# A decoder block's attention stage: the third group's key projections done by seven products one stage sooner, the softmaxes queued behind the key splits

## Chip, core and metric

One core of a Trainium2 chip. The metric is the device time of one execution in microseconds. TensorE multiplies matrices, VectorE and ScalarE work element by element, GpSimd does a few side operations and issues some transfers, SyncE issues most transfers (DMA). Each of these engines runs its own queue in order; they wait for one another through semaphores.

## What is computed

One block of a decoder on 1024 tokens of width 1024, float32: an RMS norm with modulation, one wide projection, two token mixers beside each other (retention in chunks of 128 with 4 heads, and dilated window attention with 12 heads in three groups), gates that merge them, an MLP and a last norm. What matters here is the attention:

```python
ATT_GROUPS = ((128, 1), (512, 4), (2048, 16))      # window, dilation; 4 heads of 128 each
...
for gi, (win, dil) in enumerate(ATT_GROUPS):
    aq, ak, av = parts[4 + 3 * gi], parts[5 + 3 * gi], parts[6 + 3 * gi]
    o, lse = dilated_group(heads(aq, 4), heads(ak, 4), heads(av, 4), tab, win, dil)
...
wts = jax.nn.softmax(jnp.stack(lses, axis=0), axis=0)
att = jnp.einsum('gbhs,gbhsd->bshd', wts, o_all)
```

with `proj = h @ w_in` ahead of it, and in each group scores, a bias by distance, a softmax over the window, and the product with the values. The three groups' results are weighted by a softmax over their log denominators.

## The kernel before, in words

**Precision.** Every factor is split into a high and a low half (`split_w` L194, `k_split` L1484, `q_prep` L1475: ScalarE rounds the high half, VectorE subtracts it for the low half), and every product is made of three matmuls (`mm3` L203: high by low, low by high, high by high). A matmul of 128 x 128 by 512 columns is the unit.

**Stages.** First values; more values; `queries_keys` (L1212); values; the 32 chunks of retention, which also project its gates; the attention stage in two pairs of heads; then gates, output projections and the MLP.

**Seven products.** `queries_keys` projects pairs of 128-column blocks by the class `Blocks`: it works on a 2 x 2 partition of the matrices with seven products in place of eight (`ORDER` names them), each of 4 x 3 matmuls, so 84 matmuls for a pair. `PAIRS` (L1136) is the order of the pairs: r is a query or key of retention, a are two attention queries, g two gates. `a_load` (L1140) loads the weights, `a_out` (L1165) puts the results together and stores them to DRAM (`aq_d` for the queries). A plain projection, `proj_gen` (L477), takes 48 matmuls for one block.

**The attention stage.** A head is written (g, a): group g = 0, 1, 2 and head a = 0, 1 of the pair; pairs 0 and 1 follow each other. `combos` (L1751) gives the order (1,0), (1,1), (2,0), (2,1), (0,0), (0,1). In `att_step` (L1753), step i projects the keys of its head on TensorE and weaves into that, by `weave` (L493), the scores of the head before (`scores_gen` L1492; VectorE adds the bias and so empties the PSUM bank). Behind the step's matmuls come `k_split` for its keys and `scores_end` (L1526) for the head before: VectorE takes the maxima, ScalarE the exponentials of 8 blocks. Where a group is finished, `stats_out` (L1600) stores maxima and sums to DRAM and loads them back in another order.

Steps 6 to 9 are `cover_step` (L1791): a gate's plain projection covers other work. Step n = 0 (gate 0) takes the scores of (0,1), splits values, ends the softmax, makes the weights of the groups (`weights` L1608) and scales the probabilities of group 0 (`pscale` L1640); n = 1 (gate 1) is a projection alone; n = 2 (gate 2) weaves in transposes of the probabilities and the products with the values (`weave_pv` L1737). The first lines after each gate's matmuls copy its result out of PSUM, one half by VectorE (L1827), one by ScalarE (L1828). The PSUM pool for projections (`ps_mm`) has two buffers, which the steps take in turn, so gate 2 writes where gate 0 was; that for scores has four.

**What sets the order.** The schedule is the order of the Python calls: each engine queues its instructions as the program issues them. Loads are planned by `Steps` (L60 on): they go through three raw buffers, three ahead, and their `prep` (the splits) is put ahead of the body of the step before (`following` L114), or where a step's body calls for it ("late", or manual). `with_sums` (L576) puts a transfer that sums retention results, on GpSimd's queue, behind the second and sixth part of each projection. `u_final` (L680) scales and stores a retention head; the last is stored in the first attention step.

Of the kernel before, what the change touches and what calls it, by code (L numbers as in the profile page):

```python
# [140 lines left out]
def block_kernel(ctx, tc, io, stop=None, dbg=None):  # L141
# [433 lines left out]

    def with_sums(gen):  # L576

        return at(at(gen, 1, result_sum), 5, result_sum)

    hd = {}  # L580
    NG = H * NC
# [551 lines left out]
    r_pairs = [("r", t, h) for h in range(H) for t in "qk"]  # L1133
    a_pairs = [("a", g, p) for p in range(2) for g in range(3)]
    g_pairs = [("g", i) for i in range(len(GATES) // 2)]
    PAIRS = [{"r": r_pairs, "a": a_pairs, "g": g_pairs}[i].pop(0) for i in "rargrargrargrargaa"]  # L1136
    NA = len(PAIRS)
    OA = {}

    def a_load(q, part):  # L1140
        pair = PAIRS[q]
        src = io[{"g": "w_gate2", "a": "w_aq"}.get(pair[0]) or f"w_r{pair[1]}"]
# [22 lines left out]
    def a_out(q, n, x, y=None):  # L1165

        pair = PAIRS[q]
        if q not in OA:
            OA[q] = [x4(f"qa{q}{i}") for i in range(2)]
        i, t = int(n[0]) - 1, int(n[1]) - 1  # L1170
        o, view = OA[q][i][:, 512 * t:512 * t + 512], lambda z: z
        if pair[0] == "a" and pair[1] == 1:
            o = OA[q][i].rearrange("p (r n i) -> p r n i", r=4, n=2)[:, :, t, :]
            view = lambda z: z.rearrange("p (i r) -> p r i", r=4)
        elif pair[0] == "a" and pair[1] == 2:
            o = OA[q][i].rearrange("p (r i) -> p r i", r=8)[:, :, 64 * t:64 * t + 64]
            view = lambda z: z.rearrange("p (i r) -> p r i", r=8)
        f = AF.Sigmoid if pair[0] == "g" else AF.Copy
        if y is None:
            nc.scalar.activation(o, view(x), f)  # L1180
        else:
            (nc.vector.tensor_add if n == "12" else nc.vector.tensor_sub)(o, view(x), view(y))
            if pair[0] == "g":
                nc.scalar.activation(o, o, f)
        if n in ("12", "21"):
            if pair[0] == "g":
                dst = gate_d[GATES[2 * pair[1] + i]]
# [287 lines left out]
    def q_prep(pair, g, a):  # L1475
# [5 lines left out]
            A["q", g, a] = (hi, lo)  # L1481
        return prep

    def k_split(pair, g, a, ps):  # L1484

        hi, lo = ring(f"kh{pair}{g}{a}"), ring(f"kl{pair}{g}{a}")
        src, h_, l_ = by_blocks(ps, g), shaped(hi, g), shaped(lo, g)
        nc.scalar.copy(h_, src)
        nc.vector.tensor_sub(l_, src, fv(h_))
        A["k", g, a] = (hi, lo)  # L1490
# [109 lines left out]
    def stats_out(pair, g):  # L1600

        if g == 1:
            A["stn"] = A["p"].tile([P, 3, 8, 4], F32, tag="stn", name=f"stn{pair}")
        d = dram.tile([S, 4], F32, name=f"std{pair}{g}")
        nc.sync.dma_start(natural(d, g, 4), blocks(A["st"][:, g], g))
        nc.sync.dma_start(A["stn"][:, g], natural(d, 0, 4))

    def weights(pair):  # L1608

# [138 lines left out]
                done += 1  # L1748
        drain(main)

    combos = [(g, a) for g in (1, 2, 0) for a in range(2)]  # L1751

    def att_step(pair, i):  # L1753

        g, a = combos[i]

        def body(*args):
            ps = ps_mm(f"ak{pair}{i}")
            gen = with_sums(proj_gen(ps, args[-1]))
            if i == len(combos) - 2:  # L1760
                v_fetch(pair, 0)
            if i > 0:
                last = combos[i - 1]
                weave(gen, NK, scores_gen(pair, *last), len(SB[last[0]]), lag=2)
            elif pair == 0:
                args[0](1, True)
                for _ in range(4):
                    next(gen)
                on_T(H - 1, NC - 1)
                drain(gen)  # L1770
                u_final(H - 1)
                for h in range(H):
                    sums_left.extend(sums_of(h))
                open_att()
                args[0](3)
            else:

                gen = at(at(gen, 3, args[0]), NK - 1, lambda: k_split(pair, g, a, ps))
                weave_pv(gen, NK - 1, 0, 2)
            if i == 0:  # L1780
# [4 lines left out]
            if i > 0:  # L1785
                scores_end(pair, *last)
                if last[1] == 1:
                    stats_out(pair, last[0])
        return body

    def cover_step(pair, n):  # L1791
# [4 lines left out]
        def body(*args):  # L1796
            ps = ps_mm(f"gate0{i}")
            gen = with_sums(proj_gen(ps, args[-1]))
            if n == 0:
                v_fetch(pair, 1)  # L1800
                weave(gen, 6, scores_gen(pair, *combos[-1]), len(SB[0]), lag=2, rest=False)
                drain(gen)
                v_split(pair, 0, False)
                scores_end(pair, *combos[-1])
# [36 lines left out]
            nc.sync.dma_start(gate_d[i], t)  # L1841

    for pair in range(2):
        for i, (g, a) in enumerate(combos):
            steps.add(att_step(pair, i),
                      [wsplit(io["w_ak"][g * 4 + 2 * pair + a])] +
                      ([(aq_d[pair, *combos[i - 1]], q_prep(pair, *combos[i - 1]))] if i > 0 else []),
                      manual=("late" if pair else True) if i == 0 else False)
# [902 lines left out]
def pack(x, c, w_ada, b_ada, norm1_g, w_in, rel_bias, ret_gn_g, ret_gn_b,  # L2751
# [50 lines left out]
```

## Time and profile before

| | |
|---|---|
| three runs | 2182.73, 2183.21, 2183.33 us, median 2183.21 |
| profiled execution | 2182.64 us |
| its span, first to last instruction | 2180.9 us |
| granted TensorE clock, mean | 0.999 |
| stage of seven products | about 180 to 523 us of the span |
| attention stage, pair 0 | about 944 to 1090 us |
| attention stage, pair 1 | about 1091 to 1240 us |

Rows of the profile are read so: a line of kernel.py, an engine, an operation, the output tile, an arrow, the input tiles, shapes, a count, busy time or mean. In a timeline the first number is the start in us from the span's start, the second the time taken; brackets give the idle time before and what ended it. PE is TensorE, DVE VectorE, ACT ScalarE, POOL GpSimd, SP SyncE; a q behind the name is its queue issuing a transfer. Matmuls overlap in the pipeline, so their distance from start to start counts and not the 389 ns that one takes.

### The profile page before, as it was taken

Reading aid. Unit: us, or ns where it says so; the run is one execution under the profiler, and the core shown is the slowest. Engines: PE = TensorE matmul, PEld = TensorE weight load, DVE = VectorE, ACT = ScalarE, POOL = GpSimd, SP = SyncE. Lnnn points to the kernel's source line nnn. Section 1 sums busy time; section 2 is a strip of 40 time slices with the busy share of each in tenths; the row PEclk is TensorE's granted clock in tenths of the full one; section 3 lists DMA queues with packets and bytes.
Section 4 is the critical chain, followed back from the end, with each engine's and each line's share of the span. In section 5 each row is a group of like instructions: output and inputs, shape, how many; then the busy total and the mean of one; then the engine's idle time right before and its main releaser. Section 6 shows DMA issues by size and latency. Waiting matters only on the chain. (4 is left out here: it accounts for less than half of the span.)

```text
span 2180.9 us, 27323 instructions
## 1 busy us (share of the span) xinstructions
PE 2156.0 (99%) x10084; PEld 1791.6 (82%) x10084; DVE 1491.7 (68%) x2333; ACT 942.8 (43%) x1729; POOL 164.0 (8%) x195
## 2 busy tenths in 40 slices
PE   8999999999999999999999999999999999999998
PEld 6888888888878888888888888888778888888887
DVE  5985777774467877854655644776876665877855
ACT  5553323323434544544644625434454545533413
POOL 0001111100012212211100000001000000000003
PEclk9999999999999999999999999999999999999999
DMA  9859998844685555557763275654254435645322
GB/s 383 289 209 297 296 298 257 243 119 174 237 301 170 198 174 194 181 172 190 184 167 108 81 268 189 224 186 139 65 182 150 153 136 194 249 137 175 111 87 78
DMA packets 160881, 416.78 MB, mean 191 GB/s; under 512 B 27749, under 2 KB 55660, under 8 KB 157676
## 3 DMA queue, kind: packets, MB, share of 16 engines
q1 hardware_dynamic: 151416, 368.67, 47.9%
q0 software_dynamic: 9008, 46.14, 9.9%
q8 instruction: 79, 1.29, 0.2%
q14 instruction: 54, 0.44, 0.1%
q10 hardware_dynamic: 324, 0.23, 0.0%
HBM read 319.93 MB, written 156.13 MB: 218 GB/s over the span
## 5 line engine op out<-in xcount | busy, mean ns | idle before, releaser
L207 PE MATMUL qap<-hh,qaw 128*128 128x512 f32 x216 | 84.0, 389 | 0.0
L209 PE MATMUL qap<-hl,qaw 128*128 128x512 f32 x216 | 84.0, 389 | 0.0
L211 PE MATMUL qap<-hh,qaw 128*128 128x512 f32 x216 | 84.0, 389 | 0.0
L617 POOL TENSOR_TENSOR j<-qk,j 128x512 fp32r<-128x512 f32 x32 | 43.2, 1351 | 412.4 <-ACT j L616 393.8
L2122 POOL TENSOR_TENSOR accnf<-accnf,sqnf 128x256 f32<-128x256 f32 (+1 forms) x18 | 16.6, 922 | 609.9 <-ACT sqnf L2118 609.9
L2226 ACT ACTIVATE a<-a 128x512 f32<-128x512 f32 x48 | 30.3, 631 | 73.7 <-DVE a L2225 73.7
L1542 ACT ACTIVATE P<-P,ng 128x128 f32<-128x128 f32 (+1 forms) x96 | 42.0, 439 | 36.6 <-DVE ng L1539 36.6
L2434 ACT CAST w2h<-w2s 128x512 fp32r<-128x512 f32 x36 | 22.4, 622 | 78.7 <-DVE w2s L2472 78.7
L264 DVE TENSOR_TENSOR fw<-w1r,fw 128x512 fp32r<-128x512 f32 x48 | 32.9, 688 | 33.6 <-ACT fw L254 33.6
L1957 DVE TENSOR_TENSOR rwl<-rwl,rwh 128x1024 fp32r<-128x1024 f32 x25 | 30.2, 1220 | 29.1 <-ACT rwh L1987 29.1
L207 PE MATMUL fp<-h2h,fw 128*128 128x512 f32 x128 | 50.0, 391 | 0.0
L211 PE MATMUL fp<-h2h,fw 128*128 128x512 f32 x128 | 49.8, 389 | 0.0
L209 PE MATMUL fp<-h2l,fw 128*128 128x512 f32 x128 | 49.8, 389 | 0.0
L207 PE MATMUL roa<-rh,rwl 128*128 128x512 f32 x128 | 49.8, 389 | 0.0
L209 PE MATMUL roa<-rl,rwh 128*128 128x512 f32 x128 | 49.8, 389 | 0.0
L211 PE MATMUL roa<-rh,rwh 128*128 128x512 f32 x128 | 49.8, 389 | 0.0
L652 ACT COPY sm<-sT 128x128 f32<-128x128 f32 x32 | 8.5, 266 | 93.7 <-PE sT L640 93.7
L207 PEld LDWEIGHTS qap<-hh,qaw 128*128 128x128 f32 x216 | 40.5, 188 | 8.5
L209 PEld LDWEIGHTS qap<-hl,qaw 128*128 128x128 f32 x216 | 40.5, 188 | 8.4
L211 PEld LDWEIGHTS qap<-hh,qaw 128*128 128x128 f32 x216 | 40.5, 188 | 8.4
L2122 POOL TENSOR_TENSOR accn<-accn,sqn 128x512 f32<-128x512 f32 x12 | 15.5, 1293 | 386.1 <-ACT sqn L2118 386.1
L1947 ACT ACTIVATE rh<-rl 128x512 fp32r<-128x512 f32 x56 | 31.7, 623 | 23.4 <-PE roc L209 8.4
(3097 smaller groups left out, 7251.4 us busy)
## 6 DMA issues: line engine op xcount, KB each, us to landing
v<-vd SPq DMA_DIRECT2D x32, 512.0 KB, 4.5
raw<-in_w_ada_dram SPq DMA_DIRECT2D x32, 512.0 KB, 5.3
w1r<-in_w_ff_dram SPq DMA_DIRECT2D x32, 512.0 KB, 4.6
yt<-y POOLq DMA_DIRECT2D x24, 512.0 KB, 7.6
xsd<-as SPq DMA_DIRECT2D x24, 512.0 KB, 2.8
w2r<-in_w_ff2s_dram SPq DMA_DIRECT2D x24, 512.0 KB, 6.9
em<-in_w_ada_dram SPq DMA_DIRECT2D x16, 512.0 KB, 10.2
wrvs<-in_w_rv_dram POOLq DMA_DIRECT2D x16, 512.0 KB, 10.0
```

Source lines behind the costliest of these rows:

```text
L207: nc.tensor.matmul(o, wl, xh, start=first, stop=False, skip_group_check=skip)
L209: nc.tensor.matmul(o, wh, xl, start=False, stop=False, skip_group_check=skip)
L211: nc.tensor.matmul(o, wh, xh, start=False, stop=last, skip_group_check=skip)
L264: nc.vector.tensor_sub(t[:, 512:], src, fv(t[:, :512]))
L617: nc.gpsimd.tensor_sub(t[:, 1], src, fv(t[:, 0]))
L652: nc.scalar.copy(sm, ps[:, :C])
L1542: nc.scalar.activation(v, v, AF.Exp, bias=ng[:, blk:blk + 1], accum_out=st[:, g, blk, 2 + a:3 + a])
L1947: nc.scalar.activation(hi, fv(lo), AF.Copy, scale=sign)
L1957: nc.vector.tensor_sub(lo, fv(lo), fv(hi))
L2122: (nc.vector if f == 7 else nc.gpsimd).tensor_add(G["acc", key], G["acc", key], sq)
L2226: nc.scalar.activation(o, o, AF.Relu)
L2434: nc.scalar.copy(hi, src)
```

## The change

The keys of group 2 are no longer projected in the attention stage. Their weights are packed for seven products, two pairs (k) are put into `PAIRS`, and the results go to DRAM; the attention stage loads and splits them as it does queries. The keys of group 0 are now projected in two halves, `att_first` and `att_second`, each of four parts of the projection, and each half covers the scores of one head. `scores_end` of a head is called one step later than before, behind the loads' splits and the key split of the step (`scored`, `scores_done`). The statistics' store is issued by ScalarE, and the load back by SyncE one call later. The last four stores of retention go to GpSimd's queue, and three sums instead of two are issued in each projection.

```diff
     def with_sums(gen):
-        return at(at(gen, 1, result_sum), 5, result_sum)
+        return at(at(at(gen, 1, result_sum), 3, result_sum), 5, result_sum)
...
-    def u_final(h, es=range(4)):
+    def u_final(h, es=range(4), queue=nc.sync):
...
-            nc.sync.dma_start(y_d[h][:, 2 * (i % 2):2 * (i % 2) + 2, e // 2], t.rearrange("p (t x) -> p t x", t=2))
+            queue.dma_start(y_d[h][:, 2 * (i % 2):2 * (i % 2) + 2, e // 2], t.rearrange("p (t x) -> p t x", t=2))
...
+    ak_d = {(p, a): dram.tile([P, S], F32, name=f"akd{p}{a}") for p in range(2) for a in range(2)}
...
-    PAIRS = [{"r": r_pairs, "a": a_pairs, "g": g_pairs}[i].pop(0) for i in "rargrargrargrargaa"]
+    k_pairs = [("k", 2, p) for p in range(2)]
+    PAIRS = [{"r": r_pairs, "a": a_pairs, "g": g_pairs, "k": k_pairs}[i].pop(0) for i in "rargrarkrargrarkgaga"]
...
+            elif pair[0] == "k":
+                dst = ak_d[pair[2], i]
...
+    def k_prep(pair, a):
+        def prep(raw):
+            hi, lo = ring(f"kh{pair}2{a}"), ring(f"kl{pair}2{a}")
+            nc.scalar.copy(hi, raw)
+            nc.vector.tensor_sub(lo, raw, fv(hi))
+            A["k", 2, a] = (hi, lo)
+        return prep
...
-        d = dram.tile([S, 4], F32, name=f"std{pair}{g}")
-        nc.sync.dma_start(natural(d, g, 4), blocks(A["st"][:, g], g))
-        nc.sync.dma_start(A["stn"][:, g], natural(d, 0, 4))
+        d = A["std", g] = dram.tile([S, 4], F32, name=f"std{pair}{g}")
+        nc.scalar.dma_start(natural(d, g, 4), blocks(A["st"][:, g], g))
+
+    def stats_in():
+        for g in (1, 2):
+            if ("std", g) in A:
+                nc.sync.dma_start(A["stn"][:, g], natural(A.pop(("std", g)), 0, 4))
...
+    def scores_done():
+        while scored:
+            stats_in()
+            pair, g, a = scored.pop()
+            scores_end(pair, g, a)
+            if g > 0 and a == 1:
+                stats_out(pair, g)
...
-            if i > 0 or pair == 0:
-                k_split(pair, g, a, ps)
-            if i > 0:
-                scores_end(pair, *last)
-                if last[1] == 1:
-                    stats_out(pair, last[0])
+            if a == 1 or pair == 0:
+                k_split(pair, 1, a, ps)
+            if a == 1:
+                scored.append((pair, 1, 0))
...
+    HALF = NK // 2
+
+    def att_first(pair, a):
+        def body(*args):
+            A["kp"] = ps_mm(f"ak{pair}0{a}")
+            A["kg"] = with_sums(proj_gen(A["kp"], args[-1]))
+            done = (1, 1) if a == 0 else (2, 1)
+            args[0](1)
+            if a == 1:
+                v_fetch(pair, 0)
+            scores_done()
+            weave(itertools.islice(A["kg"], HALF), HALF, scores_gen(pair, *done), len(SB[done[0]]), lag=1)
+            scored.append((pair, *done))
+        return body
+
+    def att_second(pair, a):
+        def body(*args):
+            done = (2, 0) if a == 0 else (0, 0)
+            args[0](1)
+            weave(A["kg"], HALF, scores_gen(pair, *done), len(SB[done[0]]), lag=1)
+            k_split(pair, 0, a, A["kp"])
+            scores_done()
+            scored.append((pair, *done))
         return body
...
             if n == 0:
                 v_fetch(pair, 1)
+                scores_done()
...
+        steps.add(att_step(pair, 0), [w_load(1, 0)], manual="late" if pair else True)
+        steps.add(att_step(pair, 1), [w_load(1, 1), q_load(1, 0)])
+        steps.add(att_first(pair, 0), [w_load(0, 0), q_load(1, 1)], manual="late")
+        steps.add(att_second(pair, 0), [q_load(2, 0), k_load(0)], manual="late")
+        steps.add(att_first(pair, 1), [w_load(0, 1), q_load(2, 1), k_load(1)], manual="late")
+        steps.add(att_second(pair, 1), [q_load(0, 0)], manual="late")
         for n in range(len(COVER[pair])):
-            more = [(aq_d[pair, *combos[-1]], q_prep(pair, *combos[-1]))] if n == 0 else []
+            more = [q_load(0, 1)] if n == 0 else []
...
-        "w_ak": _cols(att[:, :, 1].reshape(1024, 1536)),
+        "w_ak": _cols(att[:, :2, 1].reshape(1024, 1024)),
+        "w_ak2": _pairs(att[:, 2, 1]),
```

On each engine's queue the changed kernel has, from the split of the keys (0,0) on: ScalarE: high half of keys (0,0), exponentials (1,1), statistics store, query (0,0), exponentials (2,0), query (0,1), gate 0's weights, keys (0,1), exponentials (2,1), statistics store, weights of gates 1 and 2, exponentials (0,0), two value casts, exponentials (0,1). VectorE: low half of keys (0,0), maxima (1,1), query (0,0), maxima (2,0), bias sums (2,1), query (0,1), gate 0's weights, bias sums (0,0), keys (0,1), maxima (2,1), weights of gates 1 and 2, maxima (0,0), bias sums (0,1), maxima (0,1), the groups' weights.

More of the change, by code (lines that the diff above doesn't have):

```diff
@@ L1141, in a_load @@
         pair = PAIRS[q]
-        src = io[{"g": "w_gate2", "a": "w_aq"}.get(pair[0]) or f"w_r{pair[1]}"]
+        src = io[{"g": "w_gate2", "a": "w_aq", "k": "w_ak2"}.get(pair[0]) or f"w_r{pair[1]}"]
         i = 2 * pair[1] + pair[2] if pair[0] == "a" else pair[-1]
@@ L1171, in a_out @@
         o, view = OA[q][i][:, 512 * t:512 * t + 512], lambda z: z
-        if pair[0] == "a" and pair[1] == 1:
+        if pair[0] in "ak" and pair[1] == 1:
             o = OA[q][i].rearrange("p (r n i) -> p r n i", r=4, n=2)[:, :, t, :]
             view = lambda z: z.rearrange("p (i r) -> p r i", r=4)
-        elif pair[0] == "a" and pair[1] == 2:
+        elif pair[0] in "ak" and pair[1] == 2:
             o = OA[q][i].rearrange("p (r i) -> p r i", r=8)[:, :, 64 * t:64 * t + 64]
@@ L1749, in weave_pv, with att_step @@
         drain(main)
-    combos = [(g, a) for g in (1, 2, 0) for a in range(2)]
-    def att_step(pair, i):
-        g, a = combos[i]
+    scored = []
+    def scores_done():
[5 more added lines that the diff above has]
+                stats_out(pair, g)
+    def att_step(pair, a):
         def body(*args):
-            ps = ps_mm(f"ak{pair}{i}")
+            ps = ps_mm(f"ak{pair}1{a}")
             gen = with_sums(proj_gen(ps, args[-1]))
-            if i == len(combos) - 2:
-                v_fetch(pair, 0)
-            if i > 0:
-                last = combos[i - 1]
-                weave(gen, NK, scores_gen(pair, *last), len(SB[last[0]]), lag=2)
+            if a == 1:
+                weave(gen, NK, scores_gen(pair, 1, 0), len(SB[1]), lag=2)
             elif pair == 0:
@@ L1770, in body @@
                 drain(gen)
-                u_final(H - 1)
+                u_final(H - 1, queue=nc.gpsimd)
                 for h in range(H):
@@ L1776, in body @@
             else:
-                gen = at(at(gen, 3, args[0]), NK - 1, lambda: k_split(pair, g, a, ps))
+                gen = at(at(gen, 3, args[0]), NK - 1, lambda: k_split(pair, 1, 0, ps))
                 weave_pv(gen, NK - 1, 0, 2)
-            if i == 0:
+            if a == 0:
                 A["st"] = A["p"].tile([P, 3, 8, 4], F32, tag="st", name=f"st{pair}")
                 bias_load(pair)
-            if i > 0 or pair == 0:
-                k_split(pair, g, a, ps)
-            if i > 0:
-                scores_end(pair, *last)
-                if last[1] == 1:
-                    stats_out(pair, last[0])
+            if a == 1 or pair == 0:
[10 more added lines that the diff above has]
+            args[0](1)
+            if a == 1:
+                v_fetch(pair, 0)
+            scores_done()
+            weave(itertools.islice(A["kg"], HALF), HALF, scores_gen(pair, *done), len(SB[done[0]]), lag=1)
+            scored.append((pair, *done))
+        return body
+    def att_second(pair, a):
[6 more added lines that the diff above has]
+            scored.append((pair, *done))
         return body
@@ L1800, in body @@
                 v_fetch(pair, 1)
-                weave(gen, 6, scores_gen(pair, *combos[-1]), len(SB[0]), lag=2, rest=False)
+                scores_done()
+                weave(gen, 6, scores_gen(pair, 0, 1), len(SB[0]), lag=2, rest=False)
                 drain(gen)
                 v_split(pair, 0, False)
-                scores_end(pair, *combos[-1])
+                scores_end(pair, 0, 1)
                 weights(pair)
@@ L1843, in block_kernel, with q_load, k_load, w_load @@
     for pair in range(2):
[L1844 to L1848, printed above, removed]
+        def q_load(g, a):
+            return aq_d[pair, g, a], q_prep(pair, g, a)
+        def k_load(a):
+            return ak_d[pair, a], k_prep(pair, a)
+        def w_load(g, a):
+            return wsplit(io["w_ak"][g * 4 + 2 * pair + a])
+        steps.add(att_step(pair, 0), [w_load(1, 0)], manual="late" if pair else True)
[4 more added lines that the diff above has]
+        steps.add(att_second(pair, 1), [q_load(0, 0)], manual="late")
         for n in range(len(COVER[pair])):
-            more = [(aq_d[pair, *combos[-1]], q_prep(pair, *combos[-1]))] if n == 0 else []
+            more = [q_load(0, 1)] if n == 0 else []
             steps.add(cover_step(pair, n), more + [wsplit(io["w_gate"][len(COVER[0]) * pair + n])], manual={2: True, 3: "late"}.get(n, False))
```

## The prediction

> **What bounds the kernel now.** I read the page first, then the list of TensorE's waits, then busy time by stretch, and last, for the attention stage, each engine in order of time.
>
> ```profile
> span 2180.9 us, 27323 instructions
> PE 2156.0 (99%) x10084; PEld 1791.6 (82%) x10084; DVE 1491.7 (68%) x2333; ACT 942.8 (43%) x1729; POOL 164.0 (8%) x195
> ```
> ```profile
> PE pb L441 <- DMA onehot<-in_onehot_dram: 5.2, 2, 3.8
> ...
> PE sc L209 <- DVE kl L1489: 0.4, 1, 0.4
> ```
> TensorE sets the time: 25 us of 2181 are left, and the attention stage's own waits are tenths. So a matmul removed is worth its pitch, and a wait put in front of TensorE costs its whole length. In the stretches below the columns are the length, then busy time of TensorE, its weight loads, VectorE, ScalarE and GpSimd, then clock and DMA.
>
> ```profile
> 180.00:523.00 343.00, 343.00 (x1515) 284.02 (x1514) 245.29 (x382) 100.01 (x174) 36.31 (x50) 1.00 0.79 238
> ```
> ```profile
> 997.29:1010.97 13.68, 13.68 (x73) 11.69 (x72) 5.04 (x6) 5.16 (x18) 1.33 (x2) 1.00 0.81 213
> 1010.97:1024.79 13.82, 13.82 (x73) 11.85 (x72) 8.27 (x11) 7.05 (x20) 1.86 (x3) 1.00 0.56 140
> 1024.79:1038.64 13.85, 13.85 (x73) 11.85 (x72) 7.60 (x13) 7.80 (x20) 1.35 (x2) 1.00 0.81 216
> 1038.64:1049.88 11.24, 11.24 (x53) 9.31 (x52) 9.15 (x29) 7.24 (x25) 0.81 (x1) 1.00 1.02 244
> ```
> The first row is the stage of seven products: 343.00/1515 = 0.2264 us from one 512-column matmul to the next. The other four are, in pair 0, the key projections of group 0 (head 0, then head 1), gate 0 and gate 1. TensorE has no gap in any of them, and VectorE and ScalarE are about half busy. What they still have to finish when TensorE reaches gate 2 is seen here, first on TensorE and then on ScalarE:
>
> ```profile
> 983.60 0.62 PE L207 MATMUL ak<-hh,raw_8244l 128*128 128x512 f32 x2
> ...
> 1049.88 0.72 PE L207 MATMUL gate<-hh,raw_8707l 128*128 128x512 f32 x2
> ```
> ```profile
> 983.85 1.01 ACT L1488 CAST kh<-ak 128x1024 fp32r<-128x1024 f32 x1 [3.85 <-PE ak L211]
> 988.08 0.40 ACT L1542 ACTIVATE P<-P,ng 128x128 f32<-128x128 f32 x1 [3.22 <-DVE ng L1539]
> ...
> 991.61 1.04 ACT L1479 ACTIVATE qh<-raw 128x1024 fp32r<-128x1024 f32 x1
> ...
> 1001.19 0.40 ACT L1542 ACTIVATE P<-P,ng 128x128 f32<-128x128 f32 x1 [2.63 <-DVE ng L1539]
> ...
> 1004.29 1.05 ACT L1479 ACTIVATE qh<-raw 128x1024 fp32r<-128x1024 f32 x1
> ...
> 1018.92 1.03 ACT L197 CAST raw_8498h<-raw 128x1024 fp32r<-128x1024 f32 x1
> 1019.86 1.05 ACT L197 CAST raw_8599h<-raw 128x1024 fp32r<-128x1024 f32 x1
> ...
> 1029.68 0.41 ACT L1542 ACTIVATE P<-P,ng 128x128 f32<-128x128 f32 x1 [3.62 <-DVE ng L1539]
> ...
> 1033.53 1.04 ACT L197 CAST raw_8707h<-raw 128x1024 fp32r<-128x1024 f32 x1
> 1034.46 2.00 ACT L1571 CAST vh<-vl 128x1024 fp32r<-128x1024 f32 x2
> 1040.64 0.40 ACT L1542 ACTIVATE P<-P,ng 128x128 f32<-128x128 f32 x1 [4.17 <-DVE ng L1539]
> ...
> 1049.23 0.59 ACT L1828 COPY g00s<-gate 128x512 f32<-128x512 f32 x1 [0.69 <-DVE g00s L1827]
> ```
> Gate 2 writes the PSUM buffer that gate 0 filled, and ScalarE's half of that copy (L1828) ends at 1049.23 + 0.59 = 1049.82, 0.06 us before gate 2's first matmul at 1049.88. Nothing was waited for, but there is no slack either: whatever makes the last softmax later against TensorE is paid by TensorE.
>
> **The matmuls.** Four key heads of group 2 leave the attention stage, 48 matmuls each, 192 x 0.2264 = 43.47 us. Two pairs of seven products enter, 2 x 7 x 12 = 168, or 38.04 us. Net -24 x 0.2264 = -5.43 us. The new pairs come at the same density as the old ones, among which VectorE has 343 - 245 = 98 us free; I cost their casts, sums and four key stores at nothing, hidden by TensorE; without that cover two pairs would cost about 245/18 = 14 us of VectorE each. The attention stage now has 21.7 us less TensorE work per pair of heads, but only two weight splits less on ScalarE and on VectorE: six key splits, six query splits, the softmaxes and the gates' weights stay.
>
> **The order on ScalarE and VectorE.** Both run in order, and the changed kernel queues on them as follows, from the split of group 0's first keys on, in each pair of heads. For each link I take the distance between two starts in the rows above and in these of VectorE:
>
> ```profile
> 984.90 1.23 DVE L1489 TENSOR_TENSOR kl<-ak,kh 128x1024 fp32r<-128x1024 f32 x1 [1.65 <-ACT kh L1488]
> 986.04 0.68 DVE L1534 TENSOR_REDUCE st<-P 128x4 f32<-128x512 f32 x1
> ...
> 992.69 1.23 DVE L1480 SCALAR_TENSOR_TENSOR ql<-raw,qh 128x1024 fp32r<-128x1024 f32 x1 [4.64 <-ACT qh L1479]
> 993.83 1.22 DVE L198 TENSOR_TENSOR raw_8378l<-raw,raw_8378h 128x1024 fp32r<-128x1024 f32 x1
> ...
> 999.74 1.21 DVE L1537 TENSOR_REDUCE st<-P 128x8 f32<-128x1024 f32 x1
> ...
> 1022.46 1.88 DVE L1519 TENSOR_TENSOR P<-sc,bias 128x512 f32<-128x512 f32 x3
> 1024.26 0.61 DVE L1523 TENSOR_TENSOR P<-sc,bias 128x256 f32<-128x256 f32 x2
> ...
> 1027.23 0.28 DVE L1529 TENSOR_REDUCE st<-P 128x1 f32<-128x128 f32 x1
> ...
> 1034.60 1.23 DVE L198 TENSOR_TENSOR raw_8707l<-raw,raw_8707h 128x1024 fp32r<-128x1024 f32 x1 [4.96 <-ACT raw_8707h L197]
> ```
> 1. Keys (0,0): high half to low half 1.05 (983.85 to 984.90), low half to the next on VectorE 1.14; maxima of (1,1) to its exponentials 2.04 (986.04 to 988.08); exponentials 3.53 (to 991.61). Sum 7.76.
> 2. ScalarE issues the store of group 1's statistics: before, SyncE did that. ScalarE's own issues in this trace are at the start:
>
> ```profile
> 0.74 0.42 ACTq L807 DMA_DIRECT2D rel<-in_rel_bias_dram  x1
> ```
> I take 0.42 (from nothing, if the queue takes it beside the next operation, to 0.6 with a wait for its own last write). Sum 8.18. The load that reads it back stays on SyncE, behind no transfer that is needed within 4 us.
> 3. Query (0,0): high to low 1.08 (991.61 to 992.69), next on VectorE 1.14, maxima of (2,0) to exponentials 1.45 (999.74 to 1001.19), exponentials 3.10 (to 1004.29). Sum 14.95.
> 4. Query (0,1): 1.08, then gate 0's weights, low half, 1.14 later; they start at 17.17 and end at 18.39. Then 1.14 to the bias sums of (0,0), 2.41 for these (1022.46 to 1024.26 + 0.61). Sum 20.72.
> 5. Low half of keys (0,1) 1.14, maxima of (2,1) to exponentials 1.45, exponentials 3.10, second statistics store 0.42. Sum 26.83.
> 6. Weights of gates 1 and 2, which stand ahead of the maxima of (0,0) on VectorE and so make them wait for ScalarE: a cast to its low half 1.07 (1033.53 to 1034.60), two low halves 2 x 1.14. Sum 30.18.
> 7. Maxima of (0,0) to exponentials 2.45 (1027.23 to 1029.68), exponentials 3.85 (to 1033.53), two value casts 1.9 (the 2.00 of their row less the overlap of neighbours). Sum 38.38. The maxima of (0,1) are ready by then (30.18 + 2.3 + 2.41 + 2.45 = 37.3).
> 8. From the exponentials of (0,1) to gate 2, as before: 9.24 (1040.64 to 1049.88). Sum 47.62.
>
> TensorE in the same time: before, 13.68 + 13.82 + 13.85 + 11.24 = 52.59 from the start of keys (0,0) to gate 2; the new path starts where these keys end, and lacks one key projection of 48 x 0.2264 = 10.87 (two halves of one remain under the scores of (2,1) and (0,0)): 41.72. The split begins 0.25 after the next stage's first matmul (983.60 to 983.85), so 41.47 are there to cover 47.62. **TensorE waits 6.15 us in each pair**: first at gate 0, whose low weights end at 18.39 where TensorE comes after 13.68 + 13.82 - 10.87 - 0.25 = 16.38, 2.0 us; the rest, 4.1 us, ahead of the transposes and gate 2. Twice: +12.3.
>
> Where does this chain start? Between the splits of keys (1,1) and (0,0) stand a query and a key of group 2, the softmax of (1,0), and a weight, a query and a key: 1.05 + 3 x 1.14 + 2.04 + 3.53 + 3 x 0.94 (1018.92 to 1019.86) = 12.9 us, against two half steps of TensorE of 5.43 + 2.81 (13.68 - 10.87), 16.5. There the queues catch up, so the chain starts on time.
>
> **The rest.** The last four retention stores move from SyncE to GpSimd, whose queue holds nothing but the sums that follow, and which read these stores last:
>
> ```profile
> yt<-y POOLq DMA_DIRECT2D x24, 512.0 KB, 7.6
> ...
> raw<-aqd SPq DMA_DIRECT2D x12, 512.0 KB, 6.3
> ```
> Landing perhaps 7.6 us after issue, they free memory that is first rewritten by the bias sums of (0,0), over 30 us later. SyncE's loads behind them were held by VectorE's query split as well, so nothing comes forward; the third sum per projection only empties the list sooner. Keys come back as queries do, 6.3 us after issue: the tightest is issued when the first key's split frees its slot, 1.14 + 2.04 + 3.53 + 2 x 0.94 - 1.23 = 7.4 us before ScalarE takes it. All this at nothing, from -0.5 (the 0.4 wait of the first scores) to +2 (a late key load).
>
> Sum: -5.43 + 12.3 = +6.9 on the profiled execution's 2182.64 (span 2180.9), 2189.5; the median of the runs is 0.57 higher, so **2190.0**.
>
> **What such a wait does to the clock.**
>
> ```profile
> 11.07 3.61 PE L846 MATMUL av<-wv0wh,hh 128*128 128x512 f32 x8 [1.70 <-ACT hh L410]
> 14.52 2.00 PE L846 MATMUL av<-wv0wh,hl 128*128 128x512 f32 x8
> 16.35 2.50 PE L846 MATMUL av<-wv0wl,hh 128*128 128x512 f32 x9
> ```
> After the idle start eight matmuls take 3.45 us, the next eight 1.83: a cold stretch loses 1.6 us. The Trainium skill ("TensorE: Matmul & The Clock Gate", Part 1: The HAM clock gate) says that the clock falls to half after one idle window of about 3.4 us, and that the windows run freely; by that rule a wait of 4.1 us can just hold one, seldom. This trace has such an idle time only at its start, so it agrees that far and shows no second fall.
>
> **Rivals.**
> - The gain stands: the operations needed at gate 2 fit in the shorter stage, the chain from the keys' split taking 41.5 us or less instead of 47.6, as it would if ScalarE's and VectorE's work ran side by side. For it: they are about half busy, and before the change nothing waits. Against: each link is a hand-over between two in-order queues. 2182.6 - 5.4 = 2177.2.
> - Only gate 0's weights are late, and later links lose their 4.1 us by overlap: -5.4 + 2 x 2.0 = -1.4, 2181.2. For it: the exponentials of (2,1) wait 5 us for VectorE. Against: the two gates' weights ahead of the maxima of (0,0) bind the queues again.
> - The waits as summed, and the clock falls in both, or a key load is late by as much: 2189.5 + 2 x 1.6 = 2192.7.
>
> **Chances.** Forecast 0.70, gain 0.08, gate 0 only 0.12, worse 0.10. The forecast's own range is 2186.5 to 2192 (statistics issues 0 to 0.6 each, hand-overs by 0.5 per pair, a late key load); with the partial case's upper part and the worse one 2184 to 2194. This kernel's measurement tells 0.2%, 4.4 us, from no change: faster 0.08 (gain stands), same 0.12 (gate 0 only), slower 0.80.
>
> **What would show it.** TensorE waits of some 2 us at gate 0 and 4 us at the first transposes or gate 2 in each pair, named by VectorE's low half and by ScalarE's scaling or copy; 24 fewer matmuls; the exponentials of (0,1) about 22 us after gate 0's due start instead of 15.8 (1024.79 to 1040.64). Wrong: no TensorE wait over 1 us there, VectorE's maxima starting before the exponentials of the step ahead have ended, or a stall in the stage of seven products.

## The result, and the profile after

The changed kernel takes 2193.36 us (median of 6 runs, 2192.64 to 2195.04) against 2183.21 (6 runs, 2182.19 to 2183.97): a ratio of 1.0048, 95% interval 1.0036 to 1.0061. That is 10.15 us slower; the forecast was 6.8 us slower. The time lies above the forecast's own range of 2186.5 to 2192 and inside the wider one of 2184 to 2194. The head of the page after, and TensorE's waits, in the columns used before (total us, times, longest us):

```profile
span 2191.5 us, 27352 instructions
PE 2156.2 (98%) x10060; PEld 1790.7 (82%) x10060; DVE 1509.5 (69%) x2361; ACT 948.9 (43%) x1743; POOL 167.8 (8%) x199
```
```profile
PE gate L207 <- ACT g00s L1876: 2.7, 1, 2.7
PE gate L207 <- ACT g04s L1876: 2.1, 1, 2.1
PE gate L207 <- DVE raw_8719l L198: 2.1, 1, 2.1
PE gate L207 <- DVE raw_9986l L198: 2.1, 1, 2.1
...
PE fp L207 <- DVE ft15h2t L293: 0.9, 1, 0.9
PE rg L207 <- DVE vr L1322: 0.8, 1, 0.8
PE pt000(0, 0, 0)_9204 L1680 <- DVE P L1663: 0.8, 1, 0.8
```
There are 24 matmuls fewer. Five of these rows are new waits at the places named beforehand: gate 0 for the low half of its weights (`raw_8719l` in pair 0, `raw_9986l` in pair 1), then the first transposes (`pt000`) and gate 2's PSUM buffer, which ScalarE's copy of gate 0 (`g00s`, `g04s`) sets free. Together they are 2.1 + 2.1 + 0.8 + 2.7 + 2.1 = 9.8 us. The rows `rg` and `ft15h2t` are new too, and stand elsewhere: `rg` at the end of the value products ahead of retention, `ft15h2t` behind the attention stage.

The links of the chain can be read from ScalarE's timeline after, pair 0 (start, length, instruction, and in brackets the idle time before it), and two rows of VectorE's:

```profile
1026.06 1.01 ACT L1501 CAST kh<-ak 128x1024 fp32r<-128x1024 f32 x1 [3.55 <-PE ak L211]
1030.29 0.40 ACT L1555 ACTIVATE P<-P,ng 128x128 f32<-128x128 f32 x1 [3.22 <-DVE ng L1552]
...
1033.94 0.67 ACTq L1618 DMA_DIRECT2D std<-st  x1
1034.66 1.06 ACT L1483 ACTIVATE qh<-raw 128x1024 fp32r<-128x1024 f32 x1 [0.75 <-ACT P L1555]
...
1049.71 0.40 ACT L1555 ACTIVATE P<-P,ng 128x128 f32<-128x128 f32 x1 [5.38 <-DVE ng L1552]
...
1052.93 0.37 ACTq L1618 DMA_DIRECT2D std<-st  x1
1053.34 1.05 ACT L197 CAST raw_8799h<-raw 128x1024 fp32r<-128x1024 f32 x1 [0.44 <-ACT P L1555]
...
1059.15 0.40 ACT L1555 ACTIVATE P<-P,ng 128x128 f32<-128x128 f32 x1 [3.81 <-DVE ng L1552]
...
1064.88 0.40 ACT L1555 ACTIVATE P<-P,ng 128x128 f32<-128x128 f32 x1
...
1070.26 2.50 ACT L1665 ACTIVATE P<-P,wt 128x256 f32<-128x256 f32 x6 [1.30 <-DVE wt L1649]
1073.46 0.58 ACT L1876 COPY g00s<-gate 128x512 f32<-128x512 f32 x1 [0.70 <-DVE g00s L1875]
```
```profile
1061.46 0.29 DVE L1542 TENSOR_REDUCE st<-P 128x1 f32<-128x128 f32 x1
...
1065.83 0.17 DVE L1636 TENSOR_TENSOR mx<-mx,stn 128x16 f32<-128x16 f32 x1 [1.86 <-DMA stn<-std]
```
From the split of keys (0,0) at 1026.06, the exponentials of (0,1) start after 1064.88 - 1026.06 = 38.82 us (worked out beforehand: 38.38). TensorE's first matmul of gate 2 starts when the copy of gate 0 ends:

```profile
1044.94 0.73 PE L207 MATMUL gate<-hh,raw_8719l 128*128 128x512 f32 x2 [2.07 <-DVE raw_8719l L198]
...
1074.10 1.18 PE L207 MATMUL gate<-hh,raw_8876l 128*128 128x512 f32 x2 [2.73 <-ACT g00s L1876]
...
1183.12 1.00 PE L207 MATMUL gate<-hh,raw_9986l 128*128 128x512 f32 x2 [2.07 <-DVE raw_9986l L198]
```
This is 1074.10 - 1026.06 = 48.04 us after the split, against 47.62 summed. Two matmuls take 0.73 us from start to end behind the first of these waits, but 1.18 and 1.00 behind the other two. The stretches after the waits show why (length, busy time of TensorE, weight loads, VectorE, ScalarE, GpSimd, then the granted clock and DMA):

```profile
1042.00:1046.00 4.00, 1.93 (x12) 1.58 (x12) 3.48 (x4) 2.33 (x3) 1.09 (x2) 1.00 0.97 286
...
1074.10:1077.60 3.50, 3.50 (x10) 2.84 (x11) 1.82 (x2) 1.61 (x3) 0.00 (x0) 0.51 1.32 150
...
1183.10:1186.60 3.50, 3.48 (x9) 2.76 (x10) 3.50 (x7) 0.00 (x0) 0.00 (x0) 0.54 1.13 247
...
180.00:561.00 381.00, 381.00 (x1683) 315.49 (x1682) 268.57 (x414) 110.18 (x192) 36.22 (x50) 1.00 0.74 225
```
Behind gate 2's wait in pair 0 and behind gate 0's wait in pair 1 the clock was at half for 3.4 us, which loses 0.49 x 3.5 = 1.7 and 0.46 x 3.5 = 1.6 us; behind gate 0's wait in pair 0 it stayed at 1.00. The last row is the longer stage of seven products: 381.00/1683 = 0.2264 us per matmul, as before, with no gap.

What all this adds up to can be read without the rows of waits, from the distances between the first matmuls of the stages in the two profiled executions, which are 10.7 us apart (us; `qap` is written in the stage of seven products, `vc` by the value products behind it, `rg` in retention, `ak` by key projections, `ao` behind the attention stage):

| from, to | before | after | longer by | of this, matmuls |
|---|---|---|---|---|
| start, `qap` | 180.1 | 180.3 | 0.2 | |
| `qap`, `vc` | 342.7 | 380.8 | 38.1 | 38.0 |
| `vc`, `rg` | 108.8 | 109.7 | 0.9 | |
| `rg`, `ak` of pair 0 | 312.5 | 312.8 | 0.3 | |
| `ak`, gate 0 (pair 0) | 80.7 | 61.3 | -19.4 | -21.7 |
| gate 0, gate 2 (pair 0) | 25.1 | 29.2 | 4.1 | |
| gate 2, `ak` of pair 1 | 40.8 | 41.5 | 0.7 | |
| `ak`, gate 0 (pair 1) | 86.9 | 67.6 | -19.4 | -21.7 |
| gate 0, gate 2 (pair 1) | 25.1 | 29.1 | 4.0 | |
| gate 2, `ao` | 48.1 | 48.1 | 0.0 | |
| `ao`, end | 930.2 | 931.2 | 1.1 | |

The account: -5.4 (matmuls), 2.4 + 4.1 in pair 0 and 2.4 + 4.0 in pair 1 up to gate 2, 0.7 behind gate 2 of pair 0, 0.9 with the wait `rg`, 0.3 in retention, and 0.2 + 1.1 at the two ends: 10.7. So little of the 3.3 us at half clock comes on top of the waits. In pair 1 gate 2 starts as long after gate 0 as in pair 0, since its wait is shorter by what the slow stretch took; behind gate 2 of pair 0 only 0.7 of the 1.7 us is left. The 1.1 us behind `ao` can't be put down to the change: the same distance is 0.4 us shorter to 1.9 us longer than before's in the other profiles, the longest in run 8, which has the old matmuls.

### The profile page after: what moved, and what is told of

The parts are those of the page before. It is cut to its first block, busy times and chain, and to the rows that moved or that the text cites. A ratio compares the mean times of both kernels' runs of the same rounds, so it can differ in the third digit from the quotient of the medians.

```text
span 2191.5 us, 27352 instructions
## 1 busy us (share of the span) xinstructions
PE 2156.2 (98%) x10060; PEld 1790.7 (82%) x10060; DVE 1509.5 (69%) x2361; ACT 948.9 (43%) x1743; POOL 167.8 (8%) x199
## 3 DMA queue, kind: packets, MB, share of 16 engines
q1 hardware_dynamic: 149112, 370.70, 48.1%
## 5 line engine op out<-in xcount | busy, mean ns | idle before, releaser
L209 PE MATMUL qap<-hl,qaw 128*128 128x512 f32 x240 | 93.4, 389 | 0.0
L211 PE MATMUL qap<-hh,qaw 128*128 128x512 f32 x240 | 93.4, 389 | 0.0
L207 PE MATMUL qap<-hh,qaw 128*128 128x512 f32 x240 | 93.4, 389 | 0.0
L209 PEld LDWEIGHTS qap<-hl,qaw 128*128 128x128 f32 x240 | 45.0, 188 | 9.4
L207 PEld LDWEIGHTS qap<-hh,qaw 128*128 128x128 f32 x240 | 45.0, 188 | 9.4
L211 PEld LDWEIGHTS qap<-hh,qaw 128*128 128x128 f32 x240 | 45.0, 188 | 9.3
L2015 DVE TENSOR_TENSOR rwl<-rwl,rwh 128x1024 fp32r<-128x1024 f32 x25 | 30.2, 1220 | 29.1 <-ACT rwh L2045 29.1
L292 DVE TENSOR_TENSOR qat<-qat,qap 128x512 f32<-128x512 f32 x20 | 13.7, 687 | 46.8 <-PE qap L211 46.8
L264 DVE TENSOR_TENSOR qaw<-wa,qaw 128x512 fp32r<-128x512 f32 x60 | 39.9, 685 | 6.9 <-ACT qaw L254 6.9
```

Of the source, the lines that this page charges most:

```text
L207: nc.tensor.matmul(o, wl, xh, start=first, stop=False, skip_group_check=skip)
L209: nc.tensor.matmul(o, wh, xl, start=False, stop=False, skip_group_check=skip)
L211: nc.tensor.matmul(o, wh, xh, start=False, stop=last, skip_group_check=skip)
L264: nc.vector.tensor_sub(t[:, 512:], src, fv(t[:, :512]))
L292: nc.vector.tensor_sub(u, u, b)
L2015: nc.vector.tensor_sub(lo, fv(lo), fv(hi))
```

## The experiments

Times are medians, each beside runs of the kernel before on the same chip; its median there was 2183.17 (16 runs) for the first four and 2182.95 (27 runs) for the last four.

**1. The two moved queues put back.** Statistics and the last retention stores are issued by SyncE again, all else as in the changed kernel:

```
-        nc.scalar.dma_start(natural(d, g, 4), blocks(A["st"][:, g], g))
+        nc.sync.dma_start(natural(d, g, 4), blocks(A["st"][:, g], g))
...
-                u_final(H - 1, queue=nc.gpsimd)
+                u_final(H - 1)
```


> The changed kernel with its two moves between queues undone (statistics and the last retention stores on SyncE again). Theory A (the serial chain of ScalarE and VectorE behind the key splits makes TensorE wait at gates 0 and 2): the two statistics stores leave the chain, at most 0.95 + 0.55 us per pair by their gaps on ScalarE, so 2190.4 to 2193.4. Rival B (the moves between queues are what costs): 2185 or less. Rival C (the stage of seven products or its transfers cost the loss): 2193.

Measured: 2192.27 (2190.11 to 2193.6, 4 runs), ratio 1.004, 1.0025 to 1.0055. The waits at gate 0 fall from 2.1 to 1.6 us in each pair, so the first store costs ScalarE 0.5 us there; gate 2 then waits 2.8 and 2.7. The loss stays: the median is 1.1 us below the changed kernel's, which the two intervals don't tell from none. The moved queues are not its cause. Rival C asked for 2193, which these runs don't exclude; runs 2, 3, 5 and 6 do.

**2. Weights of gates 1 and 2 split later.** In the changed kernel VectorE has their low halves ahead of the maxima of (0,0), and ScalarE, done with the casts, idles 3.81 us for these maxima (the row at 1059.15). Here they are issued between the maxima and the exponentials of (0,0), and their loads go behind those of the statistics and values on SyncE:

```
-    def scores_end(pair, g, a):
+    def scores_end(pair, g, a, between=None):
...
         nc.vector.tensor_scalar_mul(ng, st[:, g, :, a], -1.0)
+        if between:
+            between()
...
-                scores_done()
+                scores_done(args[0])
...
-    manual={2: True, 3: "late"}.get(n, False))
+    manual={0: "late", 2: True, 3: "late"}.get(n, False))
```


> The changed kernel with the weight splits of gates 1 and 2 issued between the maxima and the exponentials of (0,0), not ahead of both. Theory A: the exponentials of (0,0) start 3.9 us sooner, those of (0,1) 3.3 us, the wait at gate 2 falls from 3.8 (2.2 in the second pair) to about 0.5 or none, the wait of 2.1 at gate 0 stays; 2185 to 2188, with one stretch of half clock gone. Rivals B and C: 2192 to 2194, as before this edit.

Measured: 2187.29 (2185.22 to 2188.89, 10 runs), ratio 1.002, 1.0011 to 1.003: 6.1 us of the 10 are back. TensorE's waits of this run, and ScalarE's exponentials of (0,0), which no longer wait:

```profile
PE gate L207 <- DVE raw_9986l L198: 2.1, 1, 2.1
PE gate L207 <- DVE raw_8719l L198: 2.1, 1, 2.1
...
PE gate L207 <- ACT g00s L1878: 0.7, 1, 0.7
...
PE gate L207 <- ACT g04s L1878: 0.4, 1, 0.4
```
```profile
1055.81 0.39 ACT L1557 ACTIVATE P<-P,ng 128x128 f32<-128x128 f32 x1
...
1069.40 2.51 ACT L1667 ACTIVATE P<-P,wt 128x256 f32<-128x256 f32 x6 [3.17 <-DVE wt L1651]
```
```profile
1065.40 0.18 DVE L1638 TENSOR_TENSOR mx<-mx,stn 128x16 f32<-128x16 f32 x1 [3.20 <-DMA stn<-std]
```
Gate 0's waits stay as they were, gate 2's nearly go. The order of work on two queues made that part of the loss; the amount of work did not change. The two pairs differ, though: from gate 0 to gate 2 pair 1 is 3.3 us shorter than after, pair 0 only 1.4. There VectorE waits 3.20 us for the second statistics, the scaling starts 0.9 us sooner than after (1069.40 against 1070.26), and gate 2's wait is short also because TensorE came late: its clock was at half for 3.41 us behind gate 0.

**3. The softmax of (1,1) ahead of the split of keys (0,0).** TensorE still works on these keys then, so the two engines do the softmax in its shadow:

```
             args[0](1)
+            if a == 0:
+                scores_done()
             weave(A["kg"], HALF, scores_gen(pair, *done), len(SB[done[0]]), lag=1)
```


> The changed kernel with one softmax, that of (1,1), ahead of the split of keys (0,0) again, in the time in which ScalarE idled 3.6 us for these keys. Theory A: everything behind it comes about 3 us sooner; no wait at gate 0, 2.5 to 3.5 us at gate 2 in each pair; 2185 to 2188. Rivals B and C: 2192 to 2194.

Measured: 2189.26 (2186.75 to 2190.37, 7 runs), ratio 1.0024, 1.0013 to 1.0035: gate 0 waits no more, but the time is above the expected 2185 to 2188. TensorE's waits in pair 0, then VectorE's and ScalarE's rows:

```profile
PE gate L207 <- ACT g00s L1878: 2.7, 1, 2.7
...
PE pt000(0, 0, 0)_9204 L1680 <- DVE P L1663: 2.6, 1, 2.6
```

```profile
1065.29 0.17 DVE L1636 TENSOR_TENSOR mx<-mx,stn 128x16 f32<-128x16 f32 x1 [4.53 <-DMA stn<-std]
```
```profile
1061.67 0.40 ACT L1555 ACTIVATE P<-P,ng 128x128 f32<-128x128 f32 x1
...
1069.29 2.50 ACT L1665 ACTIVATE P<-P,wt 128x256 f32<-128x256 f32 x6 [3.17 <-DVE wt L1649]
```
The exponentials of (0,1) do start 3.2 us sooner than after (1061.67 against 1064.88), but VectorE then waits 4.53 us for the second statistics to come back, and the scaling starts only 1.0 us sooner (1069.29 against 1070.26). In the changed kernel this load was late as well, by 1.9 us, and hidden by the exponentials. A new wait had taken the old one's place. Around gate 2 the clock was at half for 6.83 us, and from gate 2 to the keys of pair 1 pair 0 takes 42.7 us, 1.3 more than after.

**4. Two more pairs in the stage of seven products, alone.** The kernel before, with the two pairs of key heads added there and their results left unused; the attention stage computes its keys as before:

```
-    PAIRS = [... for i in "rargrargrargrargaa"]
+    k_pairs = [("k", 2, p) for p in range(2)]
+    PAIRS = [... for i in "rargrarkrargrarkgaga"]
```


> The kernel before with the two pairs of group 2's keys added to the stage of seven products, in the changed order of pairs, and their results stored but not used: the attention stage projects these keys itself as before, so the work is done twice. Theory A: TensorE's 168 matmuls and nothing else, 168 x 0.2264 = 38.0, so 2221.2, at most 1 more. Rival C: the new pairs bring 5 us or more of waits or late transfers with them, 2226 or more.

Measured: 2223.11 (2221.93 to 2224.1, 4 runs), ratio 1.0182, 1.0167 to 1.0197: 39.9 us more, where 168 matmuls are 38.0: between theory A's 2222.2 and rival C's 2226, and the interval, 36.5 to 43.0 us, reaches both. The profile decides more. This execution has the `rg` wait too:

```profile
PE rg L207 <- DVE vr L1322: 0.8, 1, 0.8
```
In the distances of the table above, `qap` to `vc` is 38.1 us longer than before, `vc` to `rg` 0.9, and from `ak` of pair 0 to `ao` no row differs from before's by more than 0.02. The rest of its 40.6 us is 0.5 ahead of `qap`, 0.1 in retention and 1.1 behind `ao`, in the two ends that vary without the new pairs as well. So the new pairs bring 0.9 us with them. The distance from `vc` to `rg` is 109.74 us in every profile with the new pairs and 108.80 in the two without.

**5 and 6. Both moves; and both with the load issued sooner.** Run 5 has the edits of 2 and 3. Run 6 adds the load of the second statistics ahead of the two value loads on SyncE:

```
+                stats_in()
                 v_fetch(pair, 1)
                 scores_done(args[0])
```


> The changed kernel with both moves: the weight splits of gates 1 and 2 behind the exponentials' inputs of (0,0), and the softmax of (1,1) ahead of the split of keys (0,0). Theory A (the +10 us is the chain of ScalarE and VectorE up to gate 2, in pair 0 in part the late load of the second statistics): gate 0 does not wait; in pair 0 gate 2 and its transposes still wait 2 to 5 us, since the load of the statistics lands no sooner, and VectorE waits for it by 3 to 5 us; in pair 1 gate 2 waits under 1 us. Time 2180 to 2185. Theory B (the two moves are two ways to the same 6 us and don't add): no better than the weight splits alone, 2187 or more. Theory C (a part of the 10 us has nothing to do with the chain): 2187 or more with no wait at gate 2.

> As the run with both moves, and the load of the second statistics issued on SyncE ahead of the two value loads. Theory A: VectorE's wait for the statistics falls to under 1.5 us, gate 2 waits under 1 us in both pairs, the TensorE clock stays full there, and the time is 2177 to 2180, 3 to 6 us below before: the 24 matmuls saved stand. Theory B (the load isn't what the weights wait for in the end): the same time as the run with both moves. Rival C (SyncE's queue stands still for the store of the statistics and the gate's weights and values come late): slower than the run with both moves, with a DMA named at gate 1, gate 2 or the values' casts.

Measured: 2179.3 (2178.9 to 2182.15, 11 runs) and 2179.65 (2178.62 to 2181.46, 11 runs), ratios 0.9985, 0.9976 to 0.9994, and 0.9985, 0.9976 to 0.9993. Both are faster than the kernel before and some 14 us faster than the changed one. The 24 matmuls saved now show: 2182.95 - 5.4 + 0.9 = 2178.4, and the two times lie 0.9 and 1.2 us above that. Neither profile has a half clock in the attention stage. Run 5's profile differs from what was expected in the place: pair 0 had no wait for the statistics, pair 1 had. First run 5, VectorE and then TensorE, then the same of run 6:

```profile
1193.48 0.17 DVE L1638 TENSOR_TENSOR mx<-mx,stn 128x16 f32<-128x16 f32 x1 [3.65 <-DMA stn<-std]
```
```profile
PE gate L207 <- ACT g04s L1880: 2.7, 1, 2.7
```
```profile
1191.41 0.18 DVE L1638 TENSOR_TENSOR mx<-mx,stn 128x16 f32<-128x16 f32 x1 [1.26 <-DMA stn<-std]
```
```profile
PE gate L207 <- ACT g04s L1881: 0.2, 1, 0.2
```
The profiled execution of run 5 took 2182.15, as one other of the 11 did; the remaining nine lie between 2178.9 and 2179.94. So that late load is probably there in some executions only (one of the two slow ones has a profile), and issuing it sooner changes the median by nothing that can be told.

**7. The run of 3, with the load ahead of the value loads.** The edit of 3 and the line of 6:

> The run with the softmax of (1,1) ahead of the split of keys (0,0) (2189.3, where pair 0 waited 5.6 us and VectorE 4.5 us for the second statistics), with the load of those statistics issued ahead of the two value loads and nothing else. Theory A (that load is why it gained 3 us less than expected): VectorE waits at most 1.5 us for it, pair 0's wait falls from 5.6 to 2 to 3.5 us, time 2185.5 to 2187.5. Theory B (the wait for the load only hid another one that ends as late): 2188.5 to 2190 with the same wait at gate 2.

Measured: 2188.8 (2185.22 to 2189.87, 10 runs), ratio 1.0023, 1.0014 to 1.0032. That is run 3 again within its spread, and above theory A's 2185.5 to 2187.5, though three of the ten executions took 2185.2 to 2185.6. VectorE still waits 3.08 us in pair 0, 1.5 less than in run 3, and the transposes start 1.5 us sooner behind gate 0. In this execution the clock took that back: in pair 1 it was at half for 6.83 us around gate 2, not 3.41, and gate 2 to `ao` took 49.9 us against 48.5. SyncE's issues tell why VectorE still waits, here in run 7, with VectorE's row, and then in run 5:

```profile
1053.42 1.46 SPq L85 DMA_DIRECT2D raw<-in_w_ak_dram  x2
1054.98 0.40 SPq L1624 DMA_DIRECT2D stn<-std  x1
```
```profile
1064.79 0.17 DVE L1636 TENSOR_TENSOR mx<-mx,stn 128x16 f32<-128x16 f32 x1 [3.08 <-DMA stn<-std]
```
```profile
1054.61 0.38 SPq L1626 DMA_DIRECT2D stn<-std  x1
1055.09 1.00 SPq L85 DMA_DIRECT2D raw<-in_w_ak_dram  x2
```
In run 7 the load is issued at nearly the same time, but behind two weight loads of 512 KB each, and VectorE's use of it starts at 1064.79, 9.8 us after the issue; in run 5 it goes ahead of them and is there by 1058.25, 3.6 us after. In run 3, behind the value loads as well, it took 10.0 us (issued at 1055.32, used at 1065.29). So the two value loads were the wrong suspects. That the weight loads are the right ones is what this comparison suggests; pair 1 of run 5, where the load also went ahead of the weights and still took 8.2 us (1185.28 to 1193.48), speaks against their being all of it. This stays open.

**8. ScalarE work put into the kernel before.** The first value cast is repeated four times ahead of the exponential of the weights, in both pairs; nothing is added for TensorE:

```
+                for _ in range(4):
+                    nc.scalar.copy(A["v", 0, 0][0], fv(A["l", 0, 0]))
                 weights(pair)
```


> The kernel before with ScalarE's cast of the first value tile repeated four times, just ahead of the exponential of the weights, in both pairs: 4 x about 1.0 us = 4.0 to 4.2 us of ScalarE per pair and nothing for TensorE. Theory A (the chain to gate 2 had no slack in the kernel before: its copy of gate 0 ends at 1049.8 us, gate 2's first product starts at 1049.9): gate 2 waits 3.5 to 4.2 us per pair, +7 to +8.4, and up to 3.4 us more where a window of half clock follows; 2190.5 to 2194.5. Theory B (2 us or more of slack): at most +4.4, 2183 to 2187.5.

Measured: 2198.36 (2197.01 to 2199.34, 4 runs), ratio 1.007, 1.0056 to 1.0083, 15.4 us more: above the expected 2190.5 to 2194.5, and far from what slack would give. TensorE's waits, ScalarE's rows in pair 0, and its row of the scaling in the kernel before:

```profile
PE pt000(0, 0, 0)_9049 L1662 <- DVE P L1645: 3.1, 1, 3.1
PE pt100(0, 0, 0)_10420 L1662 <- DVE P L1645: 3.1, 1, 3.1
PE gate L207 <- ACT g04s L1830: 2.7, 1, 2.7
PE gate L207 <- ACT g00s L1830: 2.5, 1, 2.5
...
PE fp L207 <- DVE ft15h2t L293: 1.5, 1, 1.5
```
```profile
1044.24 4.28 ACT L1806 CAST vh<-vl 128x1024 fp32r<-128x1024 f32 x4
...
1052.09 2.50 ACT L1647 ACTIVATE P<-P,wt 128x256 f32<-128x256 f32 x6 [3.43 <-DVE wt L1631]
```
```profile
1046.02 2.51 ACT L1647 ACTIVATE P<-P,wt 128x256 f32<-128x256 f32 x6 [1.31 <-DVE wt L1631]
```
The scaling starts 6.07 us later than in the kernel before (1052.09 against 1046.02, where the wait for VectorE was 1.31), not 4.28: the values' low halves on VectorE, 2.35 us, must now wait for the last cast and come between the exponential and the weights. TensorE's waits of 5.6 and 5.8 us follow that shift almost whole. By the distances between the stages, gate 0 to gate 2 is 6.3 us longer in each pair, 12.6 in all. In each pair 6.83 us run at half clock, part of it under the waits themselves, and the distances behind gate 2 are 0.8 and 1.1 us longer. Another 1.9 us of this profile lie behind `ao` (the wait `ft15h2t` is there) and aren't shown to come from the casts. The chain of the kernel before had no slack: work put into it is paid by TensorE.

## Why the prediction was right

The mechanism and the direction were right, the size was low: 10.15 us measured, 6.8 forecast. In the two profiles the pairs of heads cost 13.5 us where 12.3 were forecast (12.8 up to gate 2, 0.7 behind it); 0.9 came with the wait `rg`, 0.3 in retention, and 1.3 at the two ends, which vary from run to run.

**The matmuls.** Right: 10060 against 10084, at 0.2264 us in the longer stage too.

**The chain of ScalarE and VectorE.** Right in mechanism, place and nearly in size. Its sums to the exponentials of (0,1), 38.38, and to gate 2, 47.62, measured 38.82 and 48.04. Gate 0's wait of 2.0 was 2.1 in both pairs; the 4.1 ahead of transposes and gate 2 was 3.5 in pair 0 and 2.1 in pair 1, where TensorE came later because its clock was at half. Runs 2, 3, 5 and 6 took waits away by order alone, and in runs 5 and 6 the time came within 1.2 us of what the saved matmuls give; run 8 brought the same waits into the kernel before. The 0.44 us by which the chain came out longer are those of the first statistics store. It was taken at 0.42, between nothing and 0.6; the next query starts 4.37 us behind the start of the exponentials (1034.66 - 1030.29) where 3.53 were taken without a store, so it cost 0.84. The second cost 0.53 (1053.34 - 1049.71 = 3.63 against 3.10). In run 1, without the stores on ScalarE, gate 0's waits are 0.5 us shorter. One of the signs named as wrong did appear, at one link: VectorE's maxima of (0,1) start at 1061.46, and the exponentials of (0,0) run to the casts at 1063.00. The prediction's own sum had it so: these maxima from 34.9, those exponentials until 36.5.

**The clock.** The forecast's sum had nothing for it, and the rival that had it (2192.7) got 0.10. The clock did fall in both pairs, by 3.3 us of lost time, close to the 2 x 1.6 of that rival; and the measured 2193.36 is nearer to it than to the forecast. But that is luck: the losses hardly added to the waits. In pair 1 the slow stretch lay behind gate 0, where TensorE had to wait for the chain at gate 2 anyhow, and gate 2 starts 29.13 us after gate 0 as against 29.16 in pair 0. Behind gate 2 of pair 0 it cost 0.7 us. The Trainium skill ("TensorE: Matmul & The Clock Gate", Part 1: The HAM clock gate) has the clock fall after one idle window of about 3.4 us. The half-clock stretches here are that long, 3.41 us; but pair 1's followed a wait of 2.07 us, so a window idle from end to end isn't needed, and the prediction's "seldom", drawn from that rule, was too mild.

**The stage of seven products at nothing.** Mis-sized: the wait `rg` comes with the new pairs, 0.9 us in every profile that has them. It lies inside the bounds given for the rest (up to +2), but these had a late key load in mind, and none was seen.

**The load of the statistics.** The step said that it is behind no transfer needed within 4 us. That was wrong: after, VectorE waited 1.9 us for it in pair 0 (the row at 1065.83). It cost nothing here, because the exponentials of (0,1) ended later still; in run 3, with these sooner, it took back 2.2 of the 3.2 us gained in pair 0.

**The rivals.** "The gain stands" needed the work to run side by side; runs 5 and 6 show that it can, once two steps are put in another order, at 2179.3 to 2179.65 rather than 2177.2 (2177.8 as a median); 0.9 of the difference is the wait that the new pairs bring. "Gate 0 only" fell: run 2, which took away nearly all but gate 0's waits, is the kernel that this rival described, and took 2187.29, not 2181.2: by the distances of its profile, -5.4 + 4.8 (gate 0) + 1.7 (what is left up to gate 2) + 1.7 (a half-clock stretch behind gate 0 in pair 0) + 0.9 (`rg`) are +3.7 of its +4.1.

## What to carry to other kernels

When work leaves TensorE, look at what else had to finish in its time: sum the links of the in-order queues from one buffer hand-over to the next, since both engines can be half idle and their chain still be the longer one. Then look for links that only the order of issue makes: a split that isn't needed yet ahead of maxima that are, or a softmax behind a split whose input is late; moving two of these turned a loss of 10 us into a gain of 3.6. And when a wait on a chain is removed, look up which small load is late next.

## What the runs showed of the hardware that was not expected

- The clock can fall behind a wait of about 2 us. After waits of 2.07 us it stayed full in pair 0 and went to half in pair 1 of the same execution; a wait of 2.7 us went with no half clock in run 5, with 3.41 us of it in pair 1 of run 3, and with 6.83 us in pair 1 of run 7. In these traces the clock changes on a grid of 3.413 us (the stretches after are 1, 31, 1 and 292 times that long), and in the attention stage its falls fit how much of a wait lies in one window of the grid. The 2.07 us of pair 1 lie in one window whole; those of pair 0 are split into 0.59 and 1.48, and run 5's 2.7 into 1.33 and 1.37. In the attention stages of all ten profiles half clock followed each window at full clock with 1.98 us or more without a matmul, none with less than 1.77, and two of three in between. Near the end of the kernel it followed windows with 0.9 to 1.6 us, with matmuls still to come, so this amount is not a rule for every stage, and no run varied the place of a wait alone.
- A 16 KB load of statistics took between 3.6 and 10.0 us from its issue to its use; which other transfers make the difference stays open. In run 5 only two executions of eleven were as slow as the one in which its lateness reached TensorE.
